# Forming a weight sum with an adding DMA in the FFN pairs of a two-layer decoder trunk

## The chip, the cores and the metric

The kernel runs on one core of a Trainium2 chip. The metric is the device time of one execution in microseconds (us). The engines are TensorE (PE in the profile; its weight loads are PEld), VectorE (DVE), ScalarE (ACT), GpSimd (POOL) and SyncE (SP). The queues of SP and GpSimd issue the DMAs this text speaks of.

## The reference

Two pre-norm residual layers over a stream of 256 positions by 2048 features in float32. Layer 0 mixes with a sliding-window attention beside an mLSTM, layer 1 with a forgetting attention; each mixer is followed by a SwiGLU FFN with 5632 hidden features. The FFN is what the change is about:

```python
def swiglu(xn, w_gate, w_up, w_down):
    return (jax.nn.silu(xn @ w_gate) * (xn @ w_up)) @ w_down

for layer in range(DEPTH):
    ...
    h = h + mix.astype(h.dtype)
    h = h + swiglu(rms_norm(h, norm_ffn[layer]), w_gate[layer], w_up[layer], w_down[layer])
return rms_norm(h, norm_final)
```

## The kernel before

Every float32 operand of a large product is kept as two parts: `hi`, a rounded copy made by ScalarE, and `lo`, what is left, made by VectorE as `raw - hi`. A product is three matmuls (`three`, L532 to L534): hi by hi, lo by hi, hi by lo. The activations are the stationary side (128x128) and the weights the moving side (128 rows of the contracted dimension by 512 columns). The weights come from DRAM as raw tiles of two such blocks, 512 KB each, by `load_raw` (L134, SP's queue).

`pair_group` (L539) computes two outputs of 512 columns at once, for instance a block of `w_gate` and the same block of `w_up`, over all contracted blocks. It walks over pairs of contracted blocks in a written order (`ORDER`, `DOWN`): a pair of kind 0 is done plainly, 8 products (24 matmuls); a pair of kind 1 in seven products (21 matmuls) by a scheme of the Strassen kind, for which sums of the weights (`ta` to `td`) and of the activations (`sums_of`) are formed first. `combine` puts the products of a group together again at its end. With eight pairs in a group the kinds alternate plain and seven, and the last two are plain.

For a pair in seven products `ra` is the raw tile of the first matrix and `rb` that of the second, each with two blocks [:,0] and [:,1]. In the FFN (`halves is None`) the steps are: split `ra` whole (`hg`, `lg`); split `rb[:,1]` (`hu`, `lu`); four sums of 512 columns on VectorE, L607 to L610, two of them into a tile `t4` of their own and two over `ra`; split `t4`; split `ra`. In the odd layer's projections and in the even layer's (`halves` given) all four sums are written over `ra` and `rb`.

The order on the engines is that of a planner, which places instructions by a simulated timeline; each engine then works through its list in order and waits on semaphores. Buffers set how far ahead it can be: the operands `hi` and `lo` go into eight slots used in turn (`slot`, from the list `stock` in the FFN), and a slot is free again when TensorE has read it. A plain pair takes two slots, a pair in seven products four. Raw tiles of plain pairs have a pool of four, and those of `ra` and `rb` in the FFN a pool of `RAWS` tiles, from which `scrap` takes two before the FFN for other use. SP issues the loads in one queue, together with the DMA transposes of the hidden activations (L699).

The hidden features of a layer are done in three parts (`PARTS`): three, four and four groups of gate and up, each part followed by its share of the down projection, two groups of two outputs. In the last part of layer 1 the second two outputs are done plainly. Layer 0's FFN lies at about 300 to 1010 us of the profile, layer 1's at 1360 to 2067 us.

Of the kernel before, what the change touches and what calls it, by code (L numbers as in the profile page):

```python
# [17 lines left out]
P = 128  # L18
# [5 lines left out]
NB = 512  # L24
# [27 lines left out]
W_RAWS = 4  # L52
LATER = (6, 10, 3, 5)
LATER_DOWN = (5, 6)
RAWS = 4
P_JOIN = 4
COLD = 9
TURNED = (0,)
# [17 lines left out]
def trunk(  # L76
# [51 lines left out]
    def load_raw(w, k0, c0, n, pool=wr, bufs=4, raws=None):  # L128
        if raws:
            raw = raws.pop(0)  # L130
            raws.append(raw)
        else:
            raw = pool.tile([P, CK, NB], F32, tag="raw", name="raw", bufs=bufs)
        loaded[0] = nc.sync.dma_start(  # L134
            raw[:, :, 0:n], w[k0 * P : (k0 + CK) * P, c0 : c0 + n].rearrange("(k p) n -> p k n", p=P)
        )
        return raw
# [46 lines left out]
    def split_chunk(raw, n):  # L184
        hi, lo = slot()
        for k in (slice(0, 1), slice(1, CK)) if any(raw is f for f in fine) else (slice(0, CK),):
            latest[0] = nc.scalar.copy(hi[:, k, 0:n], raw[:, k, 0:n])  # L187
            nc.vector.tensor_tensor(  # L188
                out=lo[:, k, 0:n], in0=raw[:, k, 0:n], in1=hi[:, k, 0:n].bitcast(F32), op=ALU.subtract
            )  # L190
        return hi, lo
# [71 lines left out]
    def sums_of(pool, sh, sl, copies, full=None, tags=("tmp", "tmp"), bufs=None, box=None, x4=None):  # L263
        if box is not None:
            full, s = box[:, 0:4, :].rearrange("p (i t) q -> p i t q", i=2), box[:, 4:8, :]
            copies(full.rearrange("p i t q -> p i (t q)"))
        elif full is None:
            full = pool.tile([P, 2, NT, P], F32, tag=tags[0], name="full", bufs=bufs)
            copies(full.rearrange("p i t q -> p i (t q)"))
        if box is None:  # L270
            s = pool.tile([P, 4, P], F32, tag=tags[1], name="s4", bufs=bufs)
        nc.vector.tensor_tensor(out=s[:, 0, :], in0=full[:, 0, 1, :], in1=full[:, 1, 1, :], op=ALU.add)
        nc.vector.tensor_tensor(out=s[:, 1, :], in0=s[:, 0, :], in1=full[:, 0, 0, :], op=ALU.subtract)
        nc.vector.tensor_tensor(out=s[:, 2, :], in0=full[:, 0, 0, :], in1=full[:, 0, 1, :], op=ALU.subtract)
# [80 lines left out]
    def split_plain(dst_h, dst_l, src):  # L355
        nc.scalar.copy(dst_h, src)  # L356
        nc.vector.tensor_tensor(out=dst_l, in0=src, in1=dst_h.bitcast(F32), op=ALU.subtract)  # L357
# [181 lines left out]
    def pair_group(fp, par, lhs, sums, mats, order, todo=(), halves=None, inner=None, raws=None):  # L539
        plain = [[bank(par, "acc") for _ in range(NT)] for _ in range(2)]  # L540
        begun = set()

        def fresh(*at):
            known = at in begun
            begun.add(at)
            return not known

        todo = list(todo)
        prods = None
        kinds = [kind for kind, _ in order]  # L550
        t0, t1 = slice(0, P), slice(P, 2 * P)

        def combine(prods):
            c = fp.tile([P, 4, NB], F32, tag="c", name="c", bufs=1)
            nc.scalar.copy(c[:, 0, :], prods[0])
            if halves is None:
                nc.vector.tensor_tensor(out=c[:, 1, :], in0=prods[3], in1=c[:, 0, :], op=ALU.add)
                nc.vector.tensor_tensor(out=c[:, 2, :], in0=prods[2], in1=c[:, 1, :], op=ALU.add)
                nc.vector.tensor_tensor(
                    out=c[:, 1:4:2, :],  # L560
                    in0=prods[1].rearrange("p (a n) -> p a n", a=1).broadcast_to([P, 2, NB]),
                    in1=c[:, 1:3, :],
                    op=ALU.add,
                )
# [3 lines left out]
            nc.vector.tensor_tensor(out=c[:, 3, :], in0=prods[1], in1=c[:, 1, :], op=ALU.add)  # L568
            nc.vector.tensor_tensor(out=c[:, 2, :], in0=prods[1], in1=c[:, 2, :], op=ALU.add)
            return c  # L570

        for pos, (kind, pair) in enumerate(order):
            k0 = 2 * pair
            if inner is not None and pos == len(order) - 1:
                c = combine(prods)
                inner()
            if not kind:
                last = pos == len(order) - 1
                walk = [(i, t) for i in range(CK) for t in range(NT)]
                if last:  # L580
                    walk.sort(key=lambda it: it[1])
# [12 lines left out]
            if first:  # L594
                prods = [bank(1 - par, "prod") for _ in range(4)]
            ra, rb = (load_raw(w, k0, c0, NB, fp, W_RAWS if halves else RAWS, raws) for w, c0 in mats)
            hg, lg = split_chunk(ra, NB)
            run_due(todo, pos)
            t4 = ra if halves else fp.tile([P, 2, NB], F32, tag="t4", name="t4", bufs=1)
            ta, tb, tc_, td = (  # L600
                (ra[:, 0, :], rb[:, 0, :], rb[:, 1, :], ra[:, 1, :])
                if halves
                else (t4[:, 0, :], t4[:, 1, :], ra[:, 0, :], ra[:, 1, :])
            )
            hu, lu = slot()
            split_plain(hu[:, 1, :], lu[:, 1, :], rb[:, 1, :])
            nc.vector.tensor_tensor(out=ta, in0=rb[:, 0, :], in1=ra[:, 0, :], op=ALU.subtract)  # L607
            nc.vector.tensor_tensor(out=tb, in0=rb[:, 1, :], in1=rb[:, 0, :], op=ALU.subtract)
            nc.vector.tensor_tensor(out=tc_, in0=rb[:, 1, :], in1=ta, op=ALU.subtract)
            nc.vector.tensor_tensor(out=td, in0=ra[:, 1, :], in1=tc_, op=ALU.subtract)  # L610
            parts = []
            for src in (ra, rb) if halves else (t4, ra):
                if halves:
                    hs, ls = halves.pop(0)
                    halves.append((hs, ls))
                else:
                    hs, ls = slot()
                split_plain(hs, ls, src)
                parts.append((hs, ls))
            where = ((0, 0), (1, 0), (1, 1), (0, 1)) if halves else ((0, 0), (0, 1), (1, 0), (1, 1))  # L620
            ht = [parts[a][0][:, b, :] for a, b in where]
            lt = [parts[a][1][:, b, :] for a, b in where]
# [12 lines left out]
        return plain, c  # L635
# [741 lines left out]
```

## Time and profile before

| | us |
|---|---|
| median of 3 runs | 2077.62 |
| range of the 3 runs | 2076.95 to 2077.89 |
| the profiled execution | 2077.56 |
| its span, first to last instruction | 2075.9 |
| TensorE busy in the span | 2065.7 |
| VectorE busy | 1819.0 |
| ScalarE busy | 1373.7 |
| GpSimd busy | 44.6 |

The granted TensorE clock was 0.999 of full speed over the span. A row of the groups reads: line, engine, operation, what it writes and reads by the program's names, shapes, count, then busy us, mean ns of one, then idle us of that engine just before them and who ended it. The table of windows gives for each stretch the busy time of each engine with the number of its instructions, then the granted clock, the share of the 16 DMA engines and GB/s. A row of the timeline or the chain begins with its start in us from the span's start and its duration. In a row of waits stand the us in total, how many, and the longest.

### The profile page before, as it was taken

How to read it: one execution, taken by the hardware profiler on the slowest of the kernel's cores; microseconds unless marked ns; L12 is line 12 of the kernel's file. 1: busy time of each engine (PE TensorE's matmuls, PEld its weight loads, DVE VectorE, ACT ScalarE, POOL GpSimd, SP SyncE). 2: the span in 40 equal slices, each digit the busy share in tenths (PEclk: the TensorE clock that was granted, in tenths of full speed). 3: DMA queues.
4: the chain of work that ended last, by engine and by line, in shares of the span. 5: the costliest groups of instructions: out<-in, count | busy, mean ns of one | idle time of the engine just before them, and what ended most of it. 6: DMA issues, size and time to landing. Idle time of an engine off the chain costs nothing.

```text
span 2075.9 us, 26965 instructions
## 1 busy us (share of the span) xinstructions
PE 2065.7 (100%) x9473; PEld 1715.1 (83%) x9473; DVE 1819.0 (88%) x2367; ACT 1373.7 (66%) x1744; POOL 44.6 (2%) x66
## 2 busy tenths in 40 slices
PE   9999999999999999999999999999999999999998
PEld 7878888888888888888888888888888888888886
DVE  6788769999999999999899688689999999999994
ACT  6777678664676656667676776687655666556763
POOL 1010000000000000000000001000000000000000
PEclk9999999999999999999999999999999999999999
DMA  8566577666677666766676776586756677667764
GB/s 292 169 216 192 188 244 238 206 219 196 210 223 224 193 208 217 222 204 183 206 213 209 231 201 183 155 268 217 233 187 218 209 217 224 202 195 225 206 196 141
DMA packets 309576, 434.88 MB, mean 209 GB/s; under 512 B 106412, under 2 KB 114624, under 8 KB 309312
## 3 DMA queue, kind: packets, MB, share of 16 engines
q1 hardware_dynamic: 307088, 426.27, 66.1%
q0 software_dynamic: 1632, 5.80, 0.8%
q8 instruction: 74, 1.21, 0.2%
q10 hardware_dynamic: 720, 1.09, 0.2%
q14 instruction: 62, 0.51, 0.1%
HBM read 408.68 MB, written 2.12 MB: 198 GB/s over the span
## 4 chain that ended last, share of the span: by engine, by line
PE 97%; DVE 1%; ACT 1%; issue 1%; DMA 0%; POOLq 0%; POOL 0%; ACTq 0%; DVEq 0%
PE acc L532 21%; PE acc L534 21%; PE acc L533 21%; PE acc L223 6%; PE acc L222 6%; PE acc L224 6%; PE prod L532 5%; PE prod L533 5%; PE prod L534 5%; PE p L386 1%; PE po L487 1%; ACT s L420 0%; PE po L488 0%; DVE lo L188 0%; DMA raw<-in_w_down_dram 0%
## 5 line engine op out<-in xcount | busy, mean ns | idle before, releaser
L188 DVE TENSOR_TENSOR lo<-raw,hi 128x1024 fp32r<-128x1024 f32 (+3 forms) x656 | 771.1, 1195 | 135.5 <-ACT hi L187 133.0
L187 ACT CAST hi<-raw 128x1024 fp32r<-128x1024 f32 (+3 forms) x656 | 661.7, 1027 | 341.2 <-PE acc L534 137.2
L533 PE MATMUL acc<-lo,xh 128*128 128x512 f32 x1320 | 514.0, 389 | 0.0
L534 PE MATMUL acc<-hi,xl 128*128 128x512 f32 x1320 | 511.4, 389 | 0.0
L532 PE MATMUL acc<-hi,xh 128*128 128x512 f32 x1320 | 506.2, 390 | 0.0
L534 PEld LDWEIGHTS acc<-hi,xl 128*128 128x128 f32 x1320 | 247.8, 188 | 51.6
L533 PEld LDWEIGHTS acc<-lo,xh 128*128 128x128 f32 x1320 | 247.8, 188 | 51.4 <-issue 0.2
L532 PEld LDWEIGHTS acc<-hi,xh 128*128 128x128 f32 x1320 | 247.7, 188 | 51.3 <-issue 0.2
L356 ACT CAST hi<-raw 128x512 fp32r<-128x512 f32 x204 | 166.9, 819 | 160.7 <-PE acc L534 83.6
L357 DVE TENSOR_TENSOR lo<-raw,hi 128x512 fp32r<-128x512 f32 x204 | 191.6, 939 | 11.4 <-ACT hi L356 10.4
L533 PE MATMUL acc<-lo,mh 128*128 128x512 f32 x466 | 181.0, 389 | 0.0
L534 PE MATMUL acc<-hi,ml 128*128 128x512 f32 x466 | 180.3, 389 | 0.0
L532 PE MATMUL acc<-hi,mh 128*128 128x512 f32 x466 | 176.2, 389 | 0.1
L356 ACT CAST hi<-t 128x1024 fp32r<-128x1024 f32 x95 | 100.0, 1053 | 63.9 <-PE acc L534 38.0
L357 DVE TENSOR_TENSOR lo<-t,hi 128x1024 fp32r<-128x1024 f32 x95 | 116.2, 1224 | 15.2 <-ACT hi L356 15.0
L223 PE MATMUL acc<-lo,mh 128*128 128x512 f32 (+1 forms) x322 | 126.3, 392 | 0.0
L222 PE MATMUL acc<-hi,mh 128*128 128x512 f32 (+1 forms) x322 | 125.8, 391 | 0.0
L224 PE MATMUL acc<-hi,ml 128*128 128x512 f32 (+1 forms) x322 | 123.7, 391 | 0.0
L532 PEld LDWEIGHTS acc<-hi,mh 128*128 128x128 f32 x466 | 87.5, 188 | 18.5 <-ACT hi L187 0.5
L534 PEld LDWEIGHTS acc<-hi,ml 128*128 128x128 f32 x466 | 87.5, 188 | 18.2
L533 PEld LDWEIGHTS acc<-lo,mh 128*128 128x128 f32 x466 | 87.4, 188 | 18.2
L223 PE MATMUL acc<-lo,xh 128*128 128x512 f32 (+3 forms) x288 | 100.0, 348 | 0.2 <-DVE lo L188 0.2
(356 smaller groups left out, 3174.7 us busy)
## 6 DMA issues: line engine op xcount, KB each, us to landing
raw<-in_w_gate_dram SPq DMA_DIRECT2D x176, 512.0 KB, 4.5
raw<-in_w_up_dram SPq DMA_DIRECT2D x176, 512.0 KB, 4.6
raw<-in_w_down_dram SPq DMA_DIRECT2D x176, 512.0 KB, 4.8
raw<-in_w_in_odd_dram SPq DMA_DIRECT2D x88, 512.0 KB, 5.3
raw<-in_w_in_even_dram SPq DMA_DIRECT2D x51, 512.0 KB, 5.1
raw<-in_w_out_even_dram SPq DMA_DIRECT2D x32, 512.0 KB, 5.2
raw<-in_w_out_odd_dram SPq DMA_DIRECT2D x32, 512.0 KB, 4.7
hr<-in_w_in_even_dram SPq DMA_DIRECT2D x12, 512.0 KB, 4.5
```

The lines of the kernel that those rows point to most:

```text
L187: latest[0] = nc.scalar.copy(hi[:, k, 0:n], raw[:, k, 0:n])
L188: nc.vector.tensor_tensor(out=lo[:, k, 0:n], in0=raw[:, k, 0:n], in1=hi[:, k, 0:n].bitcast(F32), op=ALU.subtract)
L222: nc.tensor.matmul(o, ah[:, ts], hi, start=(k == 0), stop=False)
L223: nc.tensor.matmul(o, ah[:, ts], lo, start=False, stop=False)
L224: nc.tensor.matmul(o, al[:, ts], hi, start=False, stop=(k == k_all - 1 and cs.stop == n))
L356: nc.scalar.copy(dst_h, src)
L357: nc.vector.tensor_tensor(out=dst_l, in0=src, in1=dst_h.bitcast(F32), op=ALU.subtract)
L386: nc.tensor.matmul(pq[j % 2][:, j // 2, :], q_of(j, b), k_of(j)[:, 0:cols], start=True, stop=True)
L487: nc.tensor.matmul(po, v_of(j, 0), tt[:, j, 0:2, :].rearrange("p c q -> p (c q)"), start=True, stop=False)
L532: nc.tensor.matmul(o, ah, hi, start=start, stop=False)
L533: nc.tensor.matmul(o, ah, lo, start=False, stop=False)
L534: nc.tensor.matmul(o, al, hi, start=False, stop=stop)
```

## The change

In the FFN (`halves is None`) the first sum is `rb[:,0] + ra[:,0]`. It is formed by a DMA from GpSimd's queue that reads the block of the first matrix from DRAM a second time (256 KB) and adds it to `rb[:,0]` in SBUF, after the load of `rb` has landed. `rb` then holds both the sum and its own second block, and is split whole. One sum of 512 columns on VectorE (over `rb[:,1]`) and one instruction of 1024 columns (over `ra`, with a broadcast operand) form the other three. `t4` is gone and `RAWS` is 5. Signs change with it: the second operand of a product is `ra + rb` where it was `rb - ra`, so one activation sum and two additions in `combine` are subtracted the other way round. Where `halves` is given the sums stay on VectorE, four instructions as before, with the new signs.

```diff
-RAWS = 4
+RAWS = 5
...
-        nc.vector.tensor_tensor(out=s[:, 2, :], in0=full[:, 0, 0, :], in1=full[:, 0, 1, :], op=ALU.subtract)
+        nc.vector.tensor_tensor(out=s[:, 2, :], in0=full[:, 0, 1, :], in1=full[:, 0, 0, :], op=ALU.subtract)
...
                     in0=prods[1].rearrange("p (a n) -> p a n", a=1).broadcast_to([P, 2, NB]),
                     in1=c[:, 1:3, :],
-                    op=ALU.add,
+                    op=ALU.subtract,
...
             ra, rb = (load_raw(w, k0, c0, NB, fp, W_RAWS if halves else RAWS, raws) for w, c0 in mats)
+            if halves is None:
+                (w, c0), part = mats[0], slice(k0 * P, (k0 + 1) * P)
+                nc.gpsimd.dma_start(rb[:, 0, :], w[part, c0 : c0 + NB], accum_op=ALU.add)
             hg, lg = split_chunk(ra, NB)
             run_due(todo, pos)
-            t4 = ra if halves else fp.tile([P, 2, NB], F32, tag="t4", name="t4", bufs=1)
...
             hu, lu = slot()
-            split_plain(hu[:, 1, :], lu[:, 1, :], rb[:, 1, :])
-            nc.vector.tensor_tensor(out=ta, in0=rb[:, 0, :], in1=ra[:, 0, :], op=ALU.subtract)
-            nc.vector.tensor_tensor(out=tb, in0=rb[:, 1, :], in1=rb[:, 0, :], op=ALU.subtract)
-            nc.vector.tensor_tensor(out=tc_, in0=rb[:, 1, :], in1=ta, op=ALU.subtract)
-            nc.vector.tensor_tensor(out=td, in0=ra[:, 1, :], in1=tc_, op=ALU.subtract)
...
+            if halves is None:
+                split_plain(hu, lu, rb)
+                nc.vector.tensor_tensor(out=rb[:, 1, :], in0=rb[:, 0, :], in1=rb[:, 1, :], op=ALU.subtract)
+                both = rb[:, 1, :].rearrange("p (a n) -> p a n", a=1).broadcast_to([P, CK, NB])
+                nc.vector.tensor_tensor(out=ra, in0=ra, in1=both, op=ALU.subtract)
+                hc, lc = (a[:, 0, :] for a in slot())
+                split_plain(hc, lc, rb[:, 1, :])
+                hd, ld = slot()
+                split_plain(hd, ld, ra)
+                ht = [hu[:, 0, :], hd[:, 0, :], hc, hd[:, 1, :]]
+                lt = [lu[:, 0, :], ld[:, 0, :], lc, ld[:, 1, :]]
+            else:
+                split_plain(hu[:, 1, :], lu[:, 1, :], rb[:, 1, :])
+                nc.vector.tensor_tensor(out=ra[:, 0, :], in0=rb[:, 0, :], in1=ra[:, 0, :], op=ALU.add)
+                nc.vector.tensor_tensor(out=rb[:, 0, :], in0=rb[:, 1, :], in1=rb[:, 0, :], op=ALU.subtract)
+                nc.vector.tensor_tensor(out=rb[:, 1, :], in0=ra[:, 0, :], in1=rb[:, 1, :], op=ALU.subtract)
+                nc.vector.tensor_tensor(out=ra[:, 1, :], in0=ra[:, 1, :], in1=rb[:, 1, :], op=ALU.subtract)
...
```

More of the change, by code (lines that the diff above doesn't have):

```diff
@@ L567, in combine @@
             nc.vector.tensor_tensor(out=c[:, 1, :], in0=prods[2], in1=c[:, 2, :], op=ALU.add)
-            nc.vector.tensor_tensor(out=c[:, 3, :], in0=prods[1], in1=c[:, 1, :], op=ALU.add)
-            nc.vector.tensor_tensor(out=c[:, 2, :], in0=prods[1], in1=c[:, 2, :], op=ALU.add)
+            nc.vector.tensor_tensor(out=c[:, 3, :], in0=prods[1], in1=c[:, 1, :], op=ALU.subtract)
+            nc.vector.tensor_tensor(out=c[:, 2, :], in0=prods[1], in1=c[:, 2, :], op=ALU.subtract)
             return c
@@ L596, in pair_group @@
             ra, rb = (load_raw(w, k0, c0, NB, fp, W_RAWS if halves else RAWS, raws) for w, c0 in mats)
+            if halves is None:
+                (w, c0), part = mats[0], slice(k0 * P, (k0 + 1) * P)
+                nc.gpsimd.dma_start(rb[:, 0, :], w[part, c0 : c0 + NB], accum_op=ALU.add)
             hg, lg = split_chunk(ra, NB)
             run_due(todo, pos)
-            t4 = ra if halves else fp.tile([P, 2, NB], F32, tag="t4", name="t4", bufs=1)
[L600 to L604, printed above, removed]
@@ L605, in pair_group @@
-            hu, lu = slot()
-            split_plain(hu[:, 1, :], lu[:, 1, :], rb[:, 1, :])
-            nc.vector.tensor_tensor(out=ta, in0=rb[:, 0, :], in1=ra[:, 0, :], op=ALU.subtract)
-            nc.vector.tensor_tensor(out=tb, in0=rb[:, 1, :], in1=rb[:, 0, :], op=ALU.subtract)
-            nc.vector.tensor_tensor(out=tc_, in0=rb[:, 1, :], in1=ta, op=ALU.subtract)
[L610 to L613, printed above, removed]
+            hu, lu = slot()
@@ new lines, in pair_group @@
+            if halves is None:
[15 more added lines that the diff above has]
+                nc.vector.tensor_tensor(out=ra[:, 1, :], in0=ra[:, 1, :], in1=rb[:, 1, :], op=ALU.subtract)
+                parts = []
+                for src in (ra, rb):
@@ L614, in pair_group @@
                     hs, ls = halves.pop(0)
                     halves.append((hs, ls))
[L616 to L622, printed above, removed]
+                    split_plain(hs, ls, src)
+                    parts.append((hs, ls))
@@ L623, in pair_group @@
+                where = ((0, 0), (1, 0), (1, 1), (0, 1))
+                ht = [parts[a][0][:, b, :] for a, b in where]
+                lt = [parts[a][1][:, b, :] for a, b in where]
             sh, sl = sums(pair)
```

## The prediction

> **What bounds the kernel now.** I read the page's busy table and chain first: who sets the end, and how much time belongs to anyone else.
>
> ```profile
> span 2075.9 us, 26965 instructions
> PE 2065.7 (100%) x9473; PEld 1715.1 (83%) x9473; DVE 1819.0 (88%) x2367; ACT 1373.7 (66%) x1744; POOL 44.6 (2%) x66
> ...
> PE 97%; DVE 1%; ACT 1%; issue 1%; DMA 0%; POOLq 0%; POOL 0%; ACTq 0%; DVEq 0%
> ```
>
> The profiled execution took 2077.56 us, its span 2075.9; 1.7 us lie around it. The median of the three runs, 2077.62, is the same within 0.06, so the sum is made against 2077.6. The change works only inside the two FFNs, so next the busy times of FFN stretches (two of layer 0, two of layer 1).
>
> ```profile
> core 0: us, PE busy (x) PEld busy (x) DVE busy (x) ACT busy (x) POOL busy (x), PEclk, DMA share, GB/s
> 340.00:460.00 120.00, 120.00 (x532) 99.34 (x531) 116.72 (x152) 83.04 (x97) 0.00 (x0) 1.00 0.68 219
> 460.00:970.00 510.00, 509.89 (x2254) 421.90 (x2253) 479.67 (x570) 320.38 (x348) 0.00 (x0) 1.00 0.67 211
> 1330.00:1520.00 190.00, 190.00 (x841) 157.29 (x840) 169.19 (x223) 140.26 (x177) 0.70 (x1) 1.00 0.70 221
> 1520.00:1990.00 470.00, 470.00 (x2078) 389.25 (x2077) 442.33 (x528) 293.47 (x321) 0.00 (x0) 1.00 0.68 210
> ```
>
> TensorE is idle 0.11 us in 1290. VectorE comes close (116.72 of 120, or 97%, at the start of layer 0's FFN; 94% later) but not past it. A busy TensorE can hide a slow pace, so the pace itself, from the chain in order of time, and TensorE's own waits from 460 to 970 us:
>
> ```profile
> 1557.04 0.91 PE acc L532 x4
> ```
>
> ```profile
> PEld acc L532 <- ACT hi L187: 0.5, 1, 0.5
> ```
>
> Four matmuls start in 0.91 us, 227 ns each. The third row of the table above has 2254 matmuls in 510 us, 226 ns each: the whole stage runs at the pace of its undisturbed stretches, and the one wait that the profile shows there is 0.5 us. Nothing is left to win on TensorE unless there are fewer matmuls.
>
> **The change, part by part.** The seven products of a pair and their 21 matmuls stay, so TensorE's work is unchanged. What moves is the making of their operands. The prices:
>
> ```profile
> L188 DVE TENSOR_TENSOR lo<-raw,hi 128x1024 fp32r<-128x1024 f32 x620 | 746.6, 1223 | 124.2 <-ACT hi L187 121.8 <-DMA hv<-room 0.4
> ...
> L610 DVE TENSOR_TENSOR raw<-raw 128x512 f32<-128x512 f32 x109 | 75.5, 693 | 0.6
> L357 DVE TENSOR_TENSOR lo<-raw,hi 128x512 fp32r<-128x512 f32 x109 | 75.3, 691 | 10.9 <-ACT hi L356 10.4
> L356 ACT CAST hi<-raw 128x512 fp32r<-128x512 f32 x109 | 67.5, 619 | 89.9 <-PE acc L534 80.1 <-DMA raw<-in_w_in_odd_dram 3.3 <-DMA raw<-in_w_up_dram 2.6
> L607 DVE TENSOR_TENSOR t<-raw 128x512 f32<-128x512 f32 x95 | 65.6, 690 | 11.7 <-DMA raw<-in_w_down_dram 3.3 <-DMA raw<-in_w_up_dram 2.8 <-DVE lo L357 1.9
> L559 DVE TENSOR_TENSOR c<-prod,c 128x1024 f32<-128x1024 f32 x33 | 40.4, 1223 | 0.0
> ```
>
> *VectorE, per FFN pair in seven products.* Before: the low half of `ra` (1.22), of the half `rb` (0.69), four sums L607 to L610 (4 x 0.69), two full low halves (2 x 1.22): 7.1 us. After: low halves of `ra`, of the whole `rb` and of `hd` (3 x 1.22), of `hc` (0.69), one sum of 512 columns (0.69), one of 1024 (1.22; the L559 row is such an instruction, broadcast operand included): 6.3 us. Saved 0.85 us in each of 95 pairs (the count of the L607 row), 80 us of VectorE time. On the path: nothing, since VectorE ends no wait of TensorE in the rows above. ScalarE casts 1024 + 512 + 1024 + 1024 columns before and 1024 + 1024 + 512 + 1024 after: no change.
>
> *The order within the pair.* Before, L607 and L608 wrote into `t4` and could run before the `rb` cast had a slot. After, every sum waits for that cast, since it overwrites what the cast reads. From the cast to the last low half of the pair the new chain is 1.06 (cast, by the 1024-column cast below) + 1.22 + 0.69 + 1.22 + 1.06 + 1.22 = 6.5 us if nothing lies between. In the group at 590 to 620 us the old one took from 609.58 to 614.39 (rows below), 4.8 us. So about 1.6 us of lead are lost per pair. Cover: the lead that VectorE and ScalarE have on TensorE, below. The operands `hu` and `hc` are also let go one product later (3 matmuls, 0.68 us).
>
> *The adding DMA.* 95 more DMAs of 256 KB, 24.9 MB on top of 434.88 (5.7%; the DMA share of the FFN stretches, 0.67 to 0.70, goes to about 0.72, more if an addition takes an engine longer than a copy). It is issued by GpSimd, which is idle in these stretches (POOL 0.00 to 0.70 us); behind it in GpSimd's queue stand only the next adding DMAs and, at the ends of layers, `rstd` and `gf`. No run shows an adding DMA. The nearest rows:
>
> ```profile
> raw<-in_w_up_dram SPq DMA_DIRECT2D x176, 512.0 KB, 4.6
> ...
> h<-in_x_dram POOLq DMA_DIRECT2D x4, 512.0 KB, 6.9
> cb<-scratch POOLq DMA_DIRECT2D x4, 512.0 KB, 6.2
> ...
> dt__1241<-rows POOLq DMA_DIRECT2D x1, 512.0 KB, 3.8
> ...
> edge_b<-ends POOLq DMA_DIRECT2D x1, 4.0 KB, 2.9
> ```
>
> Below, a GpSimd DMA that carries almost nothing: 2.9 us from issue to landing. Above, twice the slowest 512 KB row, for an adding DMA reads its target too: 14 us, far, but no row excludes it. I take 5 us, near the plain GpSimd rows for half their bytes with a share for the addition. By the Trainium skill, "DMA: Bandwidth & Descriptors", section "Anatomy of one DMA", a GpSimd DMA is a fixed 2.0 us and bytes at 436 GB/s, 2.6 us for this one; the section says nothing of additions, and the small row (2.9 us for 4 KB) is already above it. The sum below would be the same by it.
>
> *What covers 5 us.* When does the sum have to be there? At the cast of `rb`, which waits for a slot, not for data: ScalarE's longest waits between 303 and 2063 us are for TensorE to let slots go.
>
> ```profile
> ACT hi L187 <- PE acc L534: 133.1, 88, 4.6
> ACT hi L356 <- PE acc L534: 121.6, 92, 3.0
> ```
>
> Two pairs of a steady group, as issued, cast, last low half, and used (rows of four engines; the columns are start and duration):
>
> ```profile
> 585.15 0.37 SPq L134 DMA_DIRECT2D raw<-in_w_up_dram  x1
> ...
> 598.62 0.37 SPq L134 DMA_DIRECT2D raw<-in_w_up_dram  x1
> ```
>
> ```profile
> 599.38 0.62 ACT L356 CAST hi<-raw 128x512 fp32r<-128x512 f32 x1 [1.66 <-PE acc L534]
> 600.75 1.06 ACT L356 CAST hi<-t 128x1024 fp32r<-128x1024 f32 x1 [0.75 <-PE acc L534]
> ...
> 609.58 0.62 ACT L356 CAST hi<-raw 128x512 fp32r<-128x512 f32 x1 [1.71 <-PE acc L534]
> ```
>
> ```profile
> 607.05 1.22 DVE L357 TENSOR_TENSOR lo<-raw,hi 128x1024 fp32r<-128x1024 f32 x1
> ...
> 613.17 1.22 DVE L357 TENSOR_TENSOR lo<-raw,hi 128x1024 fp32r<-128x1024 f32 x1
> ```
>
> ```profile
> 609.34 0.39 PE L532 MATMUL prod<-hi,xh 128*128 128x512 f32 x1
> ...
> 613.64 0.39 PE L533 MATMUL acc<-lo,xh 128*128 128x512 f32 x1
> ...
> 619.53 0.39 PE L532 MATMUL prod<-hi,xh 128*128 128x512 f32 x1
> ```
>
> The first pair's `rb` is issued at 585.15, lands by the median of 4.6 at 589.8 and is cast at 599.38: a window of 9.6 us. Its last low half ends at 608.27, and TensorE first needs it at 613.64: 5.4 us of lead, 3.8 after the loss of 1.6. So this sum may take 9.6 + 3.8 = 13.4 us before TensorE waits. The second pair: 603.2 to 609.58, a window of 6.4; its matmuls come 10.2 us after the first pair's, lead 9.4, or 7.8 after the loss: 14.2 us. Five us fit into the windows alone. The fifth raw tile replaces `t4` in SBUF; it lets `ra` be issued earlier and moves nothing that TensorE waits for.
>
> *The tight place.* Once per layer, at the first down projection, the chain leaves TensorE:
>
> ```profile
> 462.57 5.61 DMA raw<-in_w_down_dram
> ...
> 469.16 1.05 ACT hi L187
> ...
> 470.26 0.50 PE acc L532
> ```
>
> ```profile
> 460.08 2.86 SPq L134 DMA_DIRECT2D raw<-in_w_down_dram  x3
> ```
>
> ```profile
> 466.10 0.64 ACT L356 CAST hi<-raw 128x512 fp32r<-128x512 f32 x1
> 466.62 1.07 ACT L187 CAST hi<-raw 128x1024 fp32r<-128x1024 f32 x1
> 468.20 2.95 ACT L187 CAST hi<-raw 128x1024 fp32r<-128x1024 f32 x3 [0.50 <-DMA raw<-in_w_down_dram]
> ```
>
> Here the `rb` cast at 466.10 follows its load (issued 460.08, landed at 464.7 by the median) by 1.4 us, and stands three casts ahead of the one at 469.16 on which TensorE waits. A sum that takes 5 us lands at 469.7; three casts of 1.06 later that one starts at 472.9, 3.7 us late. With a sum of 2.9 us and a load a microsecond quicker it is no more than 0.6 late. With layer 1 the same: up to +7.4 us if ScalarE's order stays; but that order is planned anew, with the sum in it, and the freed tiles let the load start sooner. In the other direction the 0.5 us of wait quoted above can go.
>
> *Sum.* 2077.6 + 0 (VectorE's 80 us, hidden by TensorE) + 0 (adding DMAs in steady groups, hidden by windows) + between -0.5 and +7.4 at the two tight places, of which I take +0.6, near the lower end since the order there is planned anew: 2078.2.
>
> **The rivals.** (a) *The sums come late: slower.* If an adding DMA takes over 13.4 us from its load's landing, each group (22 of gate and up, 11 of down) stalls by what is over: at 15 us, 33 x 1.6 = 53 us, 2131. For it: no row prices an addition, and in the stretch from 340 to 460 VectorE at 97% leaves less lead, so there some 8 to 10 us could already cost; at 10 us, an estimate of 12 pairs by 1 us, 2090. Against it: 2.9 to 6.9 us in the GpSimd rows. Chance 0.20. (b) *The loads come late: slower.* The extra traffic and the new order stretch loads that stand in SP's one queue; one us at the start of each of the 12 gate-and-up or down sections of the two layers would be 12 us, 2090. The tight places at their worst (+7.4, 2085) belong here. For it: DMA share 0.7 already. Against it: ScalarE waits for slots, 255 us in the two rows above, far more than for loads. Chance 0.15. (c) *VectorE is the bound after all: faster.* Then 80 us go, 1997 at the least. For it: 97% busy at 340 to 460. Against it: 0.11 us of TensorE idle in 1290. Chance 0.04, most of it for a few us only. The Trainium skill's "Perfetto Trace Analysis", section "Identifying the Most-Contended Engine", wants TensorE judged by weight-load busy time and not by matmul busy time; by that TensorE stands at 83%, behind VectorE's 88%, and this case would be the likeliest. The trace disagrees: weight loads fill 421.90 of 510 us and yet matmuls start every 226 ns without a gap.
>
> **How the numbers follow.** About 0.2% (4 us) is what a measurement of this kernel tells from no change. The forecast, within 4 us, has 0.60; (a) and (b) make slower 0.35; (c) and a lucky order make faster 0.05. Alone, the forecast's range is 2077.1 (the 0.5 us won) to 2081. For 8 in 10, the lower end takes in 2 us, a fifth of the 10.2 us (2075.9 - 2065.7) in which TensorE is not busy in the whole span, 2075.5, and the upper end the early-stretch case of (a) and the case (b), 2090, which leaves out about 0.15 above and 0.04 below.
>
> **What would show it.** Right: matmuls in the FFN stretches still 226 ns apart with 95 fewer 512-column sums of three kinds, VectorE's busy time near 1739, and GpSimd DMAs of 256 KB landing in 3 to 7 us, with ScalarE's `rb` cast still released by TensorE. Wrong: that cast released by the adding DMA, TensorE waiting on L187 or L356 in every group, or the adding DMA beyond 10 us.

## The result, and the profile after

The changed kernel took 2089.74 us (median of four runs, 2087.57 to 2092.48) against 2077.76 (four runs, 2076.95 to 2078.23) of the kernel before: 1.0059 times, 95% interval 1.0041 to 1.0076, so 12 us slower. The forecast was no change (2078.2); the time lies just inside the top of the range. Two executions far out of line are left out of the comparisons below, 2291.66 us of the kernel before and 7940.88 us of e6.

The profiled execution of the changed kernel took 2087.57, the fastest of the four, 10.0 us above the profiled one of before. Its page, busy times first, then the queue of GpSimd's DMAs (packets, MB, share of 16 engines), the chain and the loads:

```profile
span 2085.9 us, 27151 instructions
PE 2069.5 (99%) x9473; PEld 1715.0 (82%) x9473; DVE 1763.7 (85%) x2177; ACT 1362.4 (65%) x1744; POOL 125.0 (6%) x161
...
q0 software_dynamic: 15312, 30.71, 7.9%
...
PE 76%; DVE 8%; ACT 6%; DMA 5%; issue 4%; SPq 1%; ACTq 0%; DVEq 0%; POOLq 0%; POOL 0%
...
raw<-in_w_gate_dram SPq DMA_DIRECT2D x176, 512.0 KB, 5.2
...
raw<-in_w_gate_dram POOLq DMA_DIRECT2D x66, 256.0 KB, 6.1
```

VectorE has 55 us less to do and TensorE the same 9473 matmuls. Yet TensorE's share of the chain fell from 97% to 76%: at some places its operands now come last. The adding DMA lands 6.1 us after its issue, and the loads on SP's queue take 5.2 instead of 4.5.

Where the time went shows in the same stretches of both kernels. The columns are the stretch, its length, busy us and instructions of TensorE, its weight loads, VectorE, ScalarE and GpSimd, the granted clock, the DMA share, and GB/s. First before, then after:

```profile
335.00:460.00 125.00, 125.00 (x554) 103.48 (x553) 121.72 (x162) 88.04 (x104) 0.00 (x0) 1.00 0.68 218
560.00:970.00 410.00, 410.00 (x1811) 339.49 (x1810) 384.88 (x460) 265.82 (x289) 0.00 (x0) 1.00 0.68 212
1375.00:1520.00 145.00, 145.00 (x643) 120.01 (x642) 137.79 (x181) 105.60 (x128) 0.70 (x1) 1.00 0.68 216
1620.00:1990.00 370.00, 370.00 (x1634) 306.39 (x1633) 347.10 (x418) 237.88 (x259) 0.00 (x0) 1.00 0.70 211
```

```profile
335.00:460.00 125.00, 123.40 (x542) 101.26 (x541) 118.25 (x145) 88.14 (x106) 7.71 (x9) 1.00 0.78 235
560.00:970.00 410.00, 409.83 (x1808) 338.71 (x1807) 364.42 (x399) 258.46 (x286) 24.77 (x29) 1.00 0.79 231
1375.00:1520.00 145.00, 142.40 (x622) 116.12 (x621) 130.34 (x159) 106.86 (x130) 9.39 (x12) 1.00 0.80 234
1620.00:1990.00 370.00, 370.00 (x1634) 306.55 (x1633) 330.17 (x363) 232.96 (x257) 23.05 (x27) 1.00 0.81 233
```

In 335 to 460 us, where layer 0's FFN starts, there are 12 matmuls fewer, at 1375 to 1520, the start of layer 1's, 21. At 227 ns each that is 7.5 us of the 10. In the two long steady stretches, 780 us with most of the adding DMAs, it is three matmuls, 0.7 us. The end of layer 0's FFN (970 to 1050 us) has six fewer, 408 for 414. The stretches with the first down projections have one fewer and one more: 444 for 445 at 460 to 560, 447 for 446 at 1520 to 1620. The busy column shows only 4.2 us for the two starts, so a TensorE that counts as busy hides part of the loss: the count tells more.

The chain of the changed kernel, in order of time, up to the first stall of layer 0:

```profile
330.63 2.52 DMA box<-box
...
340.28 1.22 DVE lo L188
...
351.00 4.70 DMA raw<-in_w_gate_dram
355.73 1.05 ACT hi L187
356.83 0.50 PE acc L532
```

Up to 338 the chain runs through the turning of the activations: ScalarE copies them out, SP's queue transposes them by DMA (`box<-box`, L317), ScalarE joins and splits them. VectorE works off a backlog from 335 to 351 without a pause; then a raw tile comes free, the load that waited for it is issued at 351.00, lands 4.70 later, is cast, and TensorE waits for that cast. Not a sum ends the wait but a plain load, issued late since its buffer came free late.

### The profile page after: what moved, and what is told of

Its sections match the earlier page's. It is cut to its first block, busy times and chain, and to the rows that moved or that the text cites. A ratio compares the mean times of both kernels' runs of the same rounds, so it can differ in the third digit from the quotient of the medians.

```text
span 2085.9 us, 27151 instructions
## 1 busy us (share of the span) xinstructions
PE 2069.5 (99%) x9473; PEld 1715.0 (82%) x9473; DVE 1763.7 (85%) x2177; ACT 1362.4 (65%) x1744; POOL 125.0 (6%) x161
## 4 chain that ended last, share of the span: by engine, by line
PE 76%; DVE 8%; ACT 6%; DMA 5%; issue 4%; SPq 1%; ACTq 0%; DVEq 0%; POOLq 0%; POOL 0%
PE acc L533 17%; PE acc L534 17%; PE acc L532 17%; PE prod L533 4%; PE prod L532 4%; PE prod L534 4%; PE acc L222 4%; PE acc L223 4%; PE acc L224 4%; DVE lo L188 3%; ACT hi L187 2%; DVE lo L357 2%; DMA raw<-in_w_down_dram 2%; DMA raw<-in_w_gate_dram 1%; DMA raw<-in_w_out_even_dram 1%
## 5 line engine op out<-in xcount | busy, mean ns | idle before, releaser
L356 ACT CAST hi<-raw 128x1024 fp32r<-128x1024 f32 (+1 forms) x299 | 265.8, 892 | 267.5 <-DVE raw L605 156.1
L357 DVE TENSOR_TENSOR lo<-raw,hi 128x1024 fp32r<-128x1024 f32 (+1 forms) x299 | 305.6, 1027 | 44.4 <-ACT hi L356 44.4
L607 DVE TENSOR_TENSOR raw<-raw 128x1024 f32<-128x1024 f32 x95 | 116.2, 1223 | 2.0
L599 POOL DMA_DIRECT2D raw<-in_w_gate_dram x66 | 56.5, 857 | 958.3 <-DMA raw<-in_w_up_dram 206.0
```

The lines of the kernel that those rows point to most:

```text
L599: nc.gpsimd.dma_start(rb[:, 0, :], w[part, c0 : c0 + NB], accum_op=ALU.add)
L607: nc.vector.tensor_tensor(out=ra, in0=ra, in1=both, op=ALU.subtract)
```

## The experiments

Each time was measured beside the kernel before on the same chip. The first four run three readings against each other: that the sums land late (L), that the extra traffic delays the loads (T), or that all sums now stand behind the cast of `rb` and lose their lead (C).

**e1: the first sum on VectorE instead of the DMA, in the new order**

```diff
-                (w, c0), part = mats[0], slice(k0 * P, (k0 + 1) * P)
-                nc.gpsimd.dma_start(rb[:, 0, :], w[part, c0 : c0 + NB], accum_op=ALU.add)
+                nc.vector.tensor_tensor(out=rb[:, 0, :], in0=rb[:, 0, :], in1=ra[:, 0, :], op=ALU.add)
```

> The changed kernel with the adding DMA taken out: the first sum is one more VectorE instruction of 512 columns over rb[:,0], everything else stays (sums over ra and rb behind the cast of rb, fifth raw tile). Theory L (the sums come late: the adding DMA lands 6.3 us after its issue and 6.9 us after its load, instead of the 5 us of the prediction) says the 12 us are gone: 2077 to 2080 us. Theory T (the 24.9 MB of extra reads delay the loads) says the same. Theory C (every sum now waits behind the cast of rb, so VectorE loses its lead at the start of each FFN) says that they stay: 2086 to 2092 us.

Measured: 2096.74 us, 1.0094 times before (1.0079 to 1.0109). No extra traffic, no adding DMA, VectorE's work as before (1817.8 us against 1819.0), and 19 us slower. So neither L nor T alone can be the reading: standing behind and in front of casts costs time without any DMA. ScalarE's waits for VectorE's sums show it. Most is now waited for the second sum (L604 in e1, L605 in the changed kernel), which overwrites a block that the cast of `rb` reads, and so stands behind that cast; before, it was for the fourth, L610. In us, times, longest wait, for e1, the changed kernel and before:

```profile
ACT hi L356 <- DVE raw L604: 190.0, 52, 7.1
```

```profile
ACT hi L356 <- DVE raw L605: 156.1, 56, 5.6
```

```profile
ACT hi L356 <- DVE raw L610: 67.2, 32, 5.0
```

C has the sign right and is short by 5 us. The run also says what the DMA is good for: with it the new path is 7 us faster than without.

**e2: the DMA copies the same bytes but does not add**

```diff
-                nc.gpsimd.dma_start(rb[:, 0, :], w[part, c0 : c0 + NB], accum_op=ALU.add)
+                nc.gpsimd.dma_start(rb[:, 0, :], w[part, c0 : c0 + NB])
```

> The changed kernel with a plain copy in place of the addition: the same DMA from GpSimd's queue, same bytes, same waits, but it overwrites rb[:,0] and so leaves out the addition of the first sum. It prices the addition by itself. If the addition makes the DMA slow, its landing falls from 6.3 us to about 4 us and its share of the DMA engines from 7.1% to about 4%; theory L then expects 2080 to 2085 us. If the landing stays near 6 us, the price is that of any GpSimd DMA beside the loads. Theories T and C expect 2087 to 2092 us either way.

Measured: 2081.67 us, 1.0020 (1.0011 to 1.0030). Every engine has its instructions in the same order as the changed kernel, and the traffic is the same 24.9 MB, so the 8 us between the two come with the addition. Landing of GpSimd's DMAs (least, median, most), the copy first; then the copy's queue:

```profile
DMA to landing us min/median/max: 3.0/4.9/6.6
```

```profile
DMA to landing us min/median/max: 4.1/6.3/8.2
```

```profile
q0 software_dynamic: 9232, 30.71, 4.6%
```

The addition makes the issue on GpSimd 0.3 us longer (853 ns for 538), the landing 1.4 us later, and costs the DMA engines nearly twice the time: the queue held 0.8% of their span before the change, so copying adds 3.8 points and adding 7.1. The other 4 us stay with a plain copy: they belong to the order and the traffic together. L's range held, those of T and C did not; but since the copy also takes less of the DMA engines, the run doesn't tell whether the addition costs because its own sum lands late or because other transfers beside it do. That is looked up in the traces below.

**e3: four raw tiles instead of five**

```diff
-RAWS = 5
+RAWS = 4
```

> The changed kernel with four raw tiles for ra and rb in place of five, the only edit. The prediction said that the fifth tile moves nothing that TensorE waits for: 2087 to 2092 us. If the loads of ra and rb now set the waits, it is slower than the changed kernel by more than 3 us.

Measured: 2087.28 us, 1.0044 (1.0029 to 1.0059). With one tile less it is 2.5 us faster if anything; the two intervals overlap. The fifth tile gives nothing.

**e4: the second sum in a tile of its own, so that it doesn't wait for the cast of `rb`**

```diff
-RAWS = 5
+RAWS = 4
...
-                nc.vector.tensor_tensor(out=rb[:, 1, :], in0=rb[:, 0, :], in1=rb[:, 1, :], op=ALU.subtract)
-                both = rb[:, 1, :].rearrange("p (a n) -> p a n", a=1).broadcast_to([P, CK, NB])
+                tq = fp.tile([P, 2, NB], F32, tag="t4", name="t4", bufs=1)[:, 0, :]
+                nc.vector.tensor_tensor(out=tq, in0=rb[:, 0, :], in1=rb[:, 1, :], op=ALU.subtract)
+                both = tq.rearrange("p (a n) -> p a n", a=1).broadcast_to([P, CK, NB])
...
-                split_plain(hc, lc, rb[:, 1, :])
+                split_plain(hc, lc, tq)
```

> The changed kernel with the second sum in a tile of its own (the room of t4, with RAWS = 4 to pay for it) instead of over rb[:,1]: the sums need the adding DMA as before but no longer wait for the cast of rb to have a slot. Theory C expects most of the 12 us gone against e3: 2078 to 2083 us. Theory L and theory T expect no change against e3: 2087 to 2092 us.

Measured: 2156.73 us, 1.0378 (1.0363 to 1.0394), 79 us slower where C expected the time of before. The sum, free of the cast, now stands early in VectorE's list, and VectorE stands still for the DMA. The chain around 684 us, and what TensorE waited for a little later:

```profile
676.05 8.04 DMA raw<-in_w_down_dram
...
684.08 0.04 DVEq L606
```

```profile
686.65 0.80 PE L533 MATMUL acc<-lo,xh 128*128 128x512 f32 x1 [4.20 <-DVE lo L188]
```

As a test of C this is void, for it brought a larger wait of its own. It shows that the cast in front of the sums was also a shelter: in e4 VectorE waits for an adding DMA 16 times, 88.3 us in all, while in the changed kernel one such DMA ends a wait, ScalarE's, of 1.3 us (row below).

**e5 and e6: the new path by place.** e5 leaves the first gate/up group of each layer (6 pairs of 95) as it was before; e6 has the new path in these six alone. `adding` chooses between the new branch and the four old sums in `t4`; both kernels have four raw tiles.

Here is e5; in e6 the two last added lines have `adding=g == 0` and `adding=False`.

```diff
-RAWS = 5
+RAWS = 4
...
-            if halves is None:
+            if halves is None and adding:
                 (w, c0), part = mats[0], slice(k0 * P, (k0 + 1) * P)
...
+            if halves is None and not adding:
+                t4 = fp.tile([P, 2, NB], F32, tag="t4", name="t4", bufs=1)
...
                     HEAVY if g in DENSE else ORDER,
                     todo,
+                    adding=g > 0,
...
-                    fp, 1 - n0 // 2, m_of, sums_d, [(wd, n0 * NB), (wd, (n0 + 1) * NB)], order, todo
+                    fp, 1 - n0 // 2, m_of, sums_d, [(wd, n0 * NB), (wd, (n0 + 1) * NB)], order, todo, adding=True
```

> The new path everywhere but in the first gate/up group of each layer (pairs 0 to 2 and 49 to 51); there the four sums are four VectorE adds through a separate tile, as before; four raw tiles. Theory A (what is lost is lost where a layer's FFN starts, because the sums lose their lead there, and the steady groups are covered): 2079 to 2082 us, and the matmuls' excess over 226.5 ns in 335-460 and 1375-1520 us falls from 2.6 and 4.5 us to under 0.5 each. Theory B (every pair pays for its slow sum, or the 25 MB of extra traffic does it): 89 of 95 pairs stay, so 2086 to 2089 us.

> The complement: the new path only in the first gate/up group of each layer (6 of 95 pairs), the four VectorE adds through a separate tile in the other 89; four raw tiles. Theory A (the starts of the two FFNs carry the loss): 2083 to 2088 us. Theory B (spread over all pairs, or traffic): 2077.5 to 2079 us.

Measured: e5 2083.16 us, 1.0028 (1.0017 to 1.0038); e6 2085.28 us, 1.0036 (1.0025 to 1.0048). Six pairs alone cost 7.5 us (0.36% of 2078), the other 89 about 5.8; e5 lies just above the 2079 to 2082 of reading A and well under the 2086 to 2089 of B. Reading B, an even share, would have given e6 0.8 us. The stalls are at their places, too: e5 has none before 460 us and e6 has this chain, where the release of a tile follows VectorE's last low half at once:

```profile
341.92 1.23 DVE lo L357
343.16 4.56 DMA raw<-in_w_up_dram
...
350.27 4.53 DMA raw<-in_w_gate_dram
...
354.88 1.05 ACT hi L187
...
355.98 0.51 PE acc L532
```

Why VectorE is late there is to be seen on the second pair, before and in e6 (VectorE's timeline; L607 and L608 are the first two of the four sums of before, L621 is the second of e6's two):

```profile
320.75 0.68 DVE L607 TENSOR_TENSOR t<-raw 128x512 f32<-128x512 f32 x1
321.35 0.69 DVE L608 TENSOR_TENSOR t<-raw 128x512 f32<-128x512 f32 x1
...
338.25 1.22 DVE L357 TENSOR_TENSOR lo<-raw,hi 128x1024 fp32r<-128x1024 f32 x1
```

```profile
332.64 1.23 DVE L357 TENSOR_TENSOR lo<-raw,hi 128x1024 fp32r<-128x1024 f32 x1 [2.15 <-ACT hi L356]
...
336.37 1.22 DVE L621 TENSOR_TENSOR raw<-raw 128x1024 f32<-128x1024 f32 x1
...
341.92 2.35 DVE L357 TENSOR_TENSOR lo<-raw,hi 128x1024 fp32r<-128x1024 f32 x2
```

Before, two of the sums were done at 322, while ScalarE was busy with the turning of the activations; the pair's last low half ended at 339.47. In e6 the sums had to wait for the cast of `rb`, which comes at 331.56, behind that turning; VectorE stood idle 2.15 us for it, and the pair's last low half ends at 343.15 (the first of the two in the last row), 3.7 us later. The sum had landed long before (its DMA was issued at 312.05, and the slowest of the six took 7.2): at this place the cast holds things up, and not the DMA. The tenth load of the gate matrix in this FFN was issued at 344.55 before, in e6 at 350.27 (in the chain above):

```profile
344.55 6.00 SPq L134 DMA_DIRECT2D raw<-in_w_gate_dram  x2
```

About half of e6's loss lies not in the starts but in the down projections behind them (at 1520 to 1620 us TensorE starts 435 matmuls against 446 of before), whose pairs are formed the old way in e6.

**e7: `rb` is loaded before `ra`**

```diff
+            if halves is None:
+                rb, ra = (load_raw(w, k0, c0, NB, fp, RAWS, raws) for w, c0 in (mats[1], mats[0]))
```

> The changed kernel with the two loads of a pair swapped, so that the tile that the adding DMA adds into lands first and the sum overlaps the second load (some 4 of its 6.9 us). Theory A (the sum comes late): the loss falls by half or more, 2078 to 2084 us. Theory B (traffic of the extra 24.9 MB, or VectorE's operations standing behind the cast): the bytes and the operations are the same, 2086 to 2091 us.

Measured: 2081.75 us, 1.0018 (1.0008 to 1.0028). With the same bytes, the same DMAs and the same operations, 8 of the 12 us are back. That is as much as leaving out the addition brought. Over the whole kernel the loads of the two gate/up matrices take 4.7 and 5.2 us by the median, against 5.2 and 5.1 in the changed kernel. But the order of the instructions also changed, and with it what the adding DMAs run beside (below), so this run alone can't say which of the two brought the 8 us.

**e9: the adding DMA reads `ra` from SBUF instead of DRAM a second time**

```diff
-                nc.gpsimd.dma_start(rb[:, 0, :], w[part, c0 : c0 + NB], accum_op=ALU.add)
+                nc.gpsimd.dma_start(rb[:, 0, :], ra[:, 0, :], accum_op=ALU.add)
```

> The changed kernel with the adding DMA reading the first matrix's block from its raw tile in SBUF rather than a second time from DRAM: same sums, same order of instructions on TensorE, VectorE, ScalarE and SyncE, 24.9 MB less read from DRAM. Theory A (the addition in the DMA is slow, where it reads from doesn't matter): landing 5.5 to 6.5 us, 2086 to 2090 us. Theory B (reading DRAM twice is what costs): landing under 5 us and loads back at 4.5 to 4.8 us, 2079 to 2083 us.

Measured: 2088.31 us, 1.0049 (1.0034 to 1.0064), the changed kernel's time. 24.9 MB less come from DRAM, TensorE, VectorE, ScalarE and SyncE keep their order, and the DMA lands no earlier:

```profile
raw<-raw POOLq DMA_DIRECT2D x95, 256.0 KB, 6.1
```

The queue's share of the DMA engines hardly falls either, 7.6% for 7.9. So reading DRAM twice costs nothing that can be measured; the price is the addition's, wherever its operand comes from.

**e10 and e11: the new path in the steady gate/up groups alone (60 pairs), and in the down projections alone (29 pairs)**

The edit is that of e5 with other values. Here is e10; in e11 they are `adding=False` and `adding=True`.

```diff
                     todo,
+                    adding=g > 0,
...
-                    fp, 1 - n0 // 2, m_of, sums_d, [(wd, n0 * NB), (wd, (n0 + 1) * NB)], order, todo
+                    fp, 1 - n0 // 2, m_of, sums_d, [(wd, n0 * NB), (wd, (n0 + 1) * NB)], order, todo, adding=False
```

> The new path only in the gate/up groups after the first of each layer (60 of 95 pairs); the first gate/up groups and all down projections with the four VectorE adds through a separate tile; four raw tiles. Theory A (the loss lies at the starts of the two FFNs and at the down projections, the steady gate/up groups are covered): within 0.1% of before, 2077 to 2080 us. Theory B (every pair costs something, or the extra traffic does): 60/95 of 12 us, about 2085 us. The saving on VectorE should again buy nothing: no theory here expects under 2077.

> The new path only in the down projections (29 of 95 pairs), the four VectorE adds elsewhere; four raw tiles. Theory A: the 5.2 us that stayed when the first groups were left out lie here, 2081 to 2084 us, in the matmuls' excess at 970-1050 and 1520-1620 us. Theory B (spread evenly): 29/95 of 12 us, 2081 to 2082 us, but as excess in all three pairs of down groups; should this run come out near 2078 the 5.2 us lie in the steady groups after all.

Measured: e10 2078.11 us, 1.0001 (0.9992 to 1.0010); e11 2082.69 us, 1.0029 (1.0017 to 1.0041). Sixty of the 95 pairs cost nothing that can be measured (-1.7 to +2.1 us), with adding DMAs that land in 5.7 us by the median and a DMA share of 0.74 to 0.78. Nor do they bring anything, with 34 us less on VectorE:

```profile
PE 2065.5 (99%) x9473; PEld 1714.7 (83%) x9473; DVE 1785.1 (86%) x2247; ACT 1366.4 (66%) x1744; POOL 96.8 (5%) x126
```

The 29 down pairs cost 6 us (3.5 to 8.5). The profile shows two stalls, 3.7 us together, one per layer at the first down projection; at 970 to 1050 us, where reading A also looked for them, there are none. TensorE's waits in e11 (us, times, longest) and the chain to the first stall:

```profile
PE acc L532 <- ACT hi L187: 3.7, 2, 2.0
```

```profile
464.00 5.74 DMA raw<-in_w_down_dram
469.77 1.05 ACT hi L187
470.86 0.50 PE acc L532
```

It is the chain that the prediction quoted from before, load, cast, TensorE, with the load issued at 464.00 instead of 462.57. This is e11's own order: the changed kernel has no such stall (its one wait between 460 and 480 us is 0.4 us, and between 1515 and 1545 it has none).

**e12 and e13: e6 and e11 with a plain copy in place of the addition**

```diff
-                nc.gpsimd.dma_start(rb[:, 0, :], w[part, c0 : c0 + NB], accum_op=ALU.add)
+                nc.gpsimd.dma_start(rb[:, 0, :], w[part, c0 : c0 + NB])
```

> The kernel with the new path in the first gate/up group of each layer alone, its six adding DMAs made plain copies of the same blocks; the order on all engines is the same. Left out: the addition in the first sum of these six pairs. Theory D (the sum's delay, 6 us instead of 5, is what these six pairs cost): 2078 to 2080 us. Theory O (the order costs it: everything behind the cast of rb, two tiles held to the end of the chain): 2083 to 2086 us as with the addition.

> The kernel with the new path in the 29 pairs of the down projections alone, its adding DMAs made plain copies; the order on all engines is the same. Left out: the addition in the first sum of these pairs. Theory D (the sum's delay): 2078 to 2080 us, TensorE's stalls at 470.9 and 1529.5 us gone. Theory O (the order): 2081 to 2084 us, the stalls stay within a third of 2.2 and 1.8 us.

Measured: e12 2084.28 us, 1.0034 (1.0020 to 1.0048); e13 2080.93 us, 1.0019 (1.0009 to 1.0028). Reading D falls at the starts: with six sums that land a microsecond earlier the time stays that of the addition, as the timeline above had it. e13 lies between the two readings, just under O's; 4 us with the copy and 6 with the addition have overlapping intervals, so what the addition costs there is not shown by the times. The stalls of e13 are still there:

```profile
PE acc L532 <- ACT hi L187: 3.0, 2, 1.7
```

At the first stall the load is issued at 463.95, as in e11, and lands after 5.00 us for 5.74: the 0.7 us that the copy saves at that place come from a load that lands sooner, not from a sum. The two runs of six pairs don't price the addition cleanly: e12 loses less at the starts than e6, and more at 1520 to 1620 us (table below), where after waits of 1.39 us and less the granted clock was 0.98 over the stretch.

**The changed kernel beside e2, instruction by instruction.** The two have the same instructions in the same order on every engine, so a wait in one can be set beside the same wait in the other. Who waited for the 95 adding DMAs of the changed kernel (us, times):

```profile
ACT hi L356: 1.3, 1
```

So the sums are hardly ever late; the six of the first groups landed 3.5 us or more before their casts began. At the starts ScalarE loses its time elsewhere: at the join of the turned activations and at the cast of a plain load. The same three instructions in the changed kernel and in e2:

```profile
331.91 2.57 ACT L322 COPY box<-box 128x1024 uint16<-128x1024 uint16 x2 [1.45 <-DMA box<-box]
...
1395.62 2.56 ACT L322 COPY box<-box 128x1024 uint16<-128x1024 uint16 x2 [1.68 <-DMA box<-box]
...
1419.86 1.04 ACT L187 CAST hi<-raw 128x1024 fp32r<-128x1024 f32 x1 [2.02 <-DMA raw<-in_w_gate_dram]
```

```profile
331.03 2.57 ACT L322 COPY box<-box 128x1024 uint16<-128x1024 uint16 x2 [0.64 <-DMA box<-box]
...
1390.35 2.57 ACT L322 COPY box<-box 128x1024 uint16<-128x1024 uint16 x2 [0.73 <-DMA box<-box]
...
1413.16 1.05 ACT L187 CAST hi<-raw 128x1024 fp32r<-128x1024 f32 x1 [0.57 <-DMA raw<-in_w_gate_dram]
```

In both kernels a GpSimd DMA is issued in the middle of these transposes (327.12 and 1390.77 us in the changed kernel). Before the change ScalarE doesn't wait at these joins at all. e9, whose DMA adds from SBUF, waits 1.41, 1.60 and 1.34 us at the three places. In e7 no GpSimd DMA is issued while the transposes run (314.61 us, then 342.15), and the waits at the joins are 0.21 us and none. The DMA engines are busy 0.78 and 0.80 of the two starts in the changed kernel, 0.72 and 0.73 in e2, 0.68 before. This is one profiled execution of each kernel, and no run varied the time of the DMA engines alone.

## Why the prediction was wrong

Where each kernel gains or loses matmuls against before, by the counts of the windows in the profiled executions (stretches in us; a matmul is about 0.23 us):

| | 335 to 460 | 460 to 560 | 970 to 1050 | 1375 to 1520 | 1520 to 1620 |
|---|---|---|---|---|---|
| changed kernel | -12 | -1 | -6 | -21 | +1 |
| e2, its copy | -7 | -2 | -1 | -4 | 0 |
| e6, six pairs | -10 | -2 | 0 | -9 | -11 |
| e12, its copy | -6 | -2 | 0 | -9 | -20 |
| e11, down pairs | +3 | -13 | +1 | +3 | -12 |
| e13, its copy | +4 | -9 | 0 | +2 | -12 |

**What held.** TensorE was the bound, and VectorE's saving bought nothing: e10 saves 34 us there and takes the time of before. The adding DMAs in steady groups are covered, as the windows of 9.6 and 6.4 us and the lead behind them had it: 60 pairs, no cost that can be measured. The term of the tight places, +0.6 with the order planned anew, held in the changed kernel: the second and the last column show one matmul fewer and one more. The forecast of the landing, 3 to 7 us, took in the median; the most was 8.2. The fifth raw tile moved nothing. The rival that VectorE is the bound after all is excluded: at 82% of weight-load busy time 55 us less work on VectorE made nothing faster. With it goes, for this kernel, what the Trainium skill ("Perfetto Trace Analysis", section "Identifying the Most-Contended Engine") says of judging TensorE by weight-load busy time; its other measure, the share of peak arithmetic, was not worked out here.

**The step that failed** is the cover: "What covers 5 us", and with it the 1.6 us of lead lost in "the order within the pair". Both were read from one steady group, at 590 to 620 us, and used for all 95 pairs. There they are right. The sum then had a term for steady groups, 0, and one for the first down projections, and none for the starts of the two FFNs, where the changed kernel loses 33 matmuls, 7.5 us of the 10. Two things are charged there.

First the order. At a start, ScalarE turns activations in the middle of a pair; the cast of `rb` stands behind that, and sums that had run ahead of the cast stand behind it too. The pair's chain ended 3.7 us later (e6), with the sum long in place, and the raw tiles held to its end came back as late loads. With a plain copy the starts still lose 11 matmuls (e2), 2.5 us of the 4 that e2 costs; its traffic is in that, so it is the most that the order can have cost there.

Second what the adding DMA takes from other transfers. The prediction asked only when its sum has to be there, priced it at 5 us (6.3 measured), and put the DMA share at about 0.72, "more if an addition takes an engine longer than a copy", without a price for that. The share at the starts was 0.78 and 0.80. The sum was late at hardly any place; the transposes and loads beside it were. With the addition the starts lose 22 matmuls more than with the copy, 5 us of the 8 between the two kernels. That other transfers are the way by which the addition costs time is read from the traces above, with e7 and e9 in agreement, and not from a run that changes nothing else. The other 3 us of the 8, the six matmuls at 970 to 1050 us among them, stay unexplained.

So the signs of being wrong did not show it. The cast of `rb` was released by the adding DMA once, TensorE did not wait in every group, and no adding DMA took 10 us: all three looked for a late sum or a loss in every group.

**The rival of late sums** had named the first of the two places (340 to 460 us) and a time of 2090, but for a DMA of 8 to 10 us whose sum comes late. The place was right; that 2089.74 came out is luck, since the sums weren't late.

**The rival of late loads** is nearer: loads take 5.2 us for 4.5, and at the starts ScalarE waits for them and for the transposes. It also gave 2090, as one us at each of 12 sections; the loss came at the starts instead, so here too the sum is luck. In steady groups the late loads are covered (e10 carries 60 of the 95 DMAs at no cost), and the second read from DRAM is not the reason (e9).

**The parts don't add up to the whole.** With the addition e6, e11 and e10 cost 7.5 + 6.0 + 0.2 = 13.7 us against 12, with the copy 7.1 + 3.9 against 4 for e2. The parts have four raw tiles, and with four the full change costs 9 (e3), so the tiles are not the difference. The table shows one: the parts lose 9 to 20 matmuls at first down projections where the full change and e2 lose at most two (e6 and e12 at that of layer 1 alone). Each run was planned anew, so the 6 us of e11 are not a part of the 12. What makes the order of the full change better there was not found, nor why e6 loses at down projections that it forms the old way.

By the Trainium skill, "DMA: Bandwidth & Descriptors", section "Anatomy of one DMA", the estimate for this transfer was 2.6 us; no GpSimd DMA of 256 KB in these runs came near it by its median, copy or addition (the fastest single copy took 3.0).

**VectorE's saving** was 55 us and not 80. It cost the forecast nothing. Nor did the lower bound of the landing, which passed over a shorter GpSimd row of the same view (1.7 us for 4 KB).

No version here beats the kernel before; e10, which keeps the new path where it is covered, equals it.

## What to carry to other kernels

Read the lead of a chain at the places where it is smallest (starts of phases, other work in the same engine's list), not in a steady group, and charge a reordering there. A sum made in place inherits every wait of the cast that reads its target, and a buffer held to the end of a longer chain comes back as a late load: look at what releases the tile of the load that TensorE waits for. An adding DMA has the price of an addition, not of its bytes: count what it takes from the shared DMA engines, and look at which transfers that are waited for run beside it, not only at when its own result is needed.

## What the runs showed of the hardware

The addition in the DMA, 256 KB: 6.3 us to landing for 4.9 of the copy, 0.85 us of issue for 0.54, and 7.1 points of the 16 DMA engines' span for 3.8 (95 of them); from SBUF in place of DRAM, 6.1 us and 6.8 points. Beside it other transfers land later: the transposes issued just after an adding DMA in the changed kernel (327.8 and 1391.3 us) took 4.1 and 4.3 us to land, those of the same place in e7, with no GpSimd DMA beside them, 2.7 and 2.5.

A stall of TensorE can be paid twice. After a stall of 4.2 us in e4 the granted clock (the third column from the right) was half, and the next 11 matmuls took 4.9 us; after some 2 us in e1, 8 matmuls took 3.5:

```profile
686.60:691.50 4.90, 4.85 (x11) 3.80 (x12) 4.90 (x6) 4.17 (x6) 0.00 (x0) 0.50 0.54 166
```

```profile
469.00:472.60 3.60, 3.54 (x8) 2.67 (x9) 3.60 (x5) 2.97 (x5) 0.00 (x0) 0.53 0.72 237
...
469.06 0.65 PE L532 MATMUL acc<-hi,mh 128*128 128x512 f32 x1 [2.06 <-ACT hi L356]
```

After the stall of e11, of like size, the clock stayed full:

```profile
470.90:474.00 3.10, 3.10 (x14) 2.57 (x15) 3.10 (x4) 3.10 (x4) 0.00 (x0) 1.00 0.81 169
```

The Trainium skill, "TensorE: Matmul & The Clock Gate", section "Part 1: The HAM clock gate (the "warmup" mystery)", has the gate close after an idle window of about 3.4 us. The 4.2 us agree; the 2.06 us of e1 are shorter than that window and yet closed it. In e12 waits of 1.39, 0.22 and 0.41 us within four us were enough: from 1532.0 to 1535.5 us the granted clock was 0.58.
